# A two-layer decoder trunk: parameter loads placed behind the first step, inputs taken by feature halves, the first weights in smaller pieces

## The chip, the cores and the metric

The kernel runs on one core of one Trainium2 chip. The metric is device time in microseconds (us) for one execution of the whole program. A profiled execution gives a trace of every instruction and transfer. The engines are PE (TensorE), DVE (VectorE), ACT (ScalarE), POOL (GpSimd) and SP (SyncE, which here only issues transfers). PEld is PE's loading of stationary operands.

## The reference: what is computed

Two layers, each a half-step SwiGLU feed-forward block, then three causal mixers side by side, then a second half-step feed-forward block. All is float32; x is 256 tokens by 1024 features.

```python
def rms_norm(x, g):
    y = x * lax.rsqrt(jnp.mean(x * x, axis=-1, keepdims=True) + RMS_EPS)
    return y * g

def swiglu(h, w13, w2):                    # w13: 1024 x 5632, w2: 2816 x 1024
    g, u = jnp.split(h @ w13, 2, axis=-1)
    return (jax.nn.silu(g) * u) @ w2

for l in range(DEPTH):                     # DEPTH = 2
    x = x + 0.5 * swiglu(rms_norm(x, norm_ffn1[l]), ffn1_w13[l], ffn1_w2[l])
    h = rms_norm(x, norm_mix[l])
    z, xbc, dt_raw, cq, ckv, kidx, widx, xl, gl = jnp.split(h @ w_in[l], offsets, axis=-1)
    y_ssd = ssd_mixer(z, xbc, dt_raw, ..., ssd_a_log[l], ssd_d[l], ssd_norm[l])
    y_att = dsa_mixer(cq, ckv, kidx, widx, ...)
    y_lru = rglru_mixer(xl, gl, ...)
    x = x + jnp.concatenate([y_ssd, y_att, y_lru], axis=-1) @ w_out[l]
    x = x + 0.5 * swiglu(rms_norm(x, norm_ffn2[l]), ffn2_w13[l], ffn2_w2[l])
```

`ssd_d` holds one skip factor for each of 8 heads; the mixers use it, as most of the small parameters, only after the first feed-forward block.

## The kernel before

x stays in SBUF as two tiles `xr` of 128 tokens (h = 0, 1) by 1024 features. A norm block (`norm_block`, one for each token half h and feature half c) has four PE transposes into one PSUM tile, four pairs of ACT and DVE instructions that write a rounded part `xh` and a remainder `xl`, and one ACT pass `nsq` over the 128 x 512 inputs for the sum of squares. The row scale (`norm_end`) is applied later.

Every float32 product is three matmuls: whi by xh, wlo by xh, whi by xl. The weights are split on the chip (`wsplit`): ACT copies a 128 x 1024 piece to a rounded `whi`, and DVE subtracts to get `wlo`. Four pairs of `whi` and `wlo` are held at a time (pool `wsplit`, 4 buffers), and four raw tiles `wraw` of 1 MB.

The first feed-forward step `ffn(..., first=True)` runs over 11 column groups c. A group takes two raw tiles (q = 0, 1: rows 0 to 511 and 512 to 1023 of the weights), each by two transfers of 512 KB (t = 0: gate columns, t = 1: up columns); each raw tile is split in two pairs, and a pair feeds 12 matmuls (2 rows of 128 by 2 token halves by 3). Then `th_s` (tanh on ACT) and `hf` (DVE) make the gated product, which PE transposes. All weight and x transfers are issued by SP in program order. A transfer that is issued takes one of 8 completion semaphores of its kind in turn, and waits for the transfer that had it before.

The small parameters are loaded by `load_params`, called in the program at group c = 1: 28 transfers, issued by POOL, with 8 semaphores of their own. `derive_params`, called at c = 8, transposes the rows collected in `stA` and `stB` into columns and computes what the mixers need. The two `dcol` transfers pick every second element of `ssd_d`, so each moves single elements of 4 bytes, repeated for 64 partitions.

Engines run their instructions in order. The order on an engine is not the program's: a scheduler at build time places each instruction by its own estimate of when it can start, so loads that are late in the program but wait for nothing come early. `issue_after` tells it to hold an instruction behind another.

Of the kernel before, what the change touches and what calls it, by code (L numbers as in the profile page):

```python
# [7 lines left out]
F32 = mybir.dt.float32  # L8
# [3 lines left out]
ALU = mybir.AluOpType  # L12
# [3 lines left out]
P = 128  # L16
DEPTH = 2
SEQ = 256
NH = SEQ // P
D = 1024  # L20
KD = D // P
DFF = 2816
# [42 lines left out]
def tile_decoder_trunk(ctx: ExitStack, tc: tile.TileContext, A: dict, out: bass.AP):  # L65
    nc = tc.nc
    V, S, G, T = nc.vector, nc.scalar, nc.gpsimd, nc.tensor

    cp = Lined(ctx.enter_context(tc.tile_pool(name="const", bufs=1)))
# [9 lines left out]
    def small_ps():  # L79
        return psm.tile([P, 512], F32, name="sm")  # L80
# [16 lines left out]
    stage = sp0.enter_context(tc.tile_pool(name="stage", bufs=1))  # L97
    g1 = stage.tile([2 * KD, P], F32, name="g1")
    S.dma_start(g1, A["norm_ffn1"].rearrange("l (m p) -> (l m) p", p=P))
    for h in range(NH):  # L100
        for c in range(2):
            nc.sync.dma_start(X[h][:, c * 512:(c + 1) * 512], x_in[0, h * P:(h + 1) * P, c * 512:(c + 1) * 512])
    gcol1 = cp.tile([P, 2 * KD], F32, name="gcol1")
    pg1 = small_ps()
# [24 lines left out]
    def cols_of(name, l0, n):  # L129
        w, r0, _ = cols[name]  # L130
        return colT[w][:, r0 + l0:r0 + l0 + n]
# [4 lines left out]
    kg = cp.tile([P, DEPTH, 64], F32, name="kg")  # L136
    kig = cp.tile([P, DEPTH, 64], F32, name="kig")
    dcol = cp.tile([P, DEPTH, 4], F32, name="dcol")
    rope = cp.tile([P, NH, 2, 16], F32, name="rope")
    wbd = cp.tile([P, 2, DEPTH, 2, P], F32, name="wbd")  # L140
    a_neg = cp.tile([P, DEPTH, 8], F32, name="a_neg")
# [62 lines left out]
    def load_params(stage):  # L204

        stA = stage.tile([P, P], F32, name="stA")
        stB = stage.tile([P, P], F32, name="stB")
        for nm, (w, r0, n) in cols.items():
            src = A[nm]
            if len(src.shape) == 2:  # L210
                ap = src.rearrange("l (m p) -> (l m) p", p=P)
            else:
                ap = src.rearrange("l k (m p) -> (l k m) p", p=P)
            G.dma_start((stA if w == 0 else stB)[r0:r0 + DEPTH * n, :], ap)
        for t, nm, n in ((a_log, "ssd_a_log", 8), (dtb, "ssd_dt_bias", 8), (qg, "q_norm", 64), (kg, "k_norm", 64),
                         (kig, "kidx_norm", 64)):
            src = A[nm]
            G.dma_start(t, bass.AP(tensor=src.tensor, offset=src.offset, ap=[[0, P], [n, DEPTH], [1, n]]))
        for r in range(2):
            src = A["ssd_d"]  # L220
            G.dma_start(dcol[64 * r:64 * r + 64], bass.AP(tensor=src.tensor, offset=src.offset + r,
                                                          ap=[[0, 64], [8, DEPTH], [2, 4]]))
        G.dma_start(rope, A["rope"].rearrange("(h p) a c -> p h a c", p=P))
        G.memset(wbd, 0.0)
        for i, nm in enumerate(("lru_wa", "lru_wi")):
            src = A[nm]
            for r in range(2):
                for l in range(DEPTH):
                    G.dma_start(wbd[64 * r:64 * r + 64, i, l, :, 64 * r:64 * r + 64],
                                src[l, r::2].rearrange("b c d -> c b d"))  # L230
        return stA, stB

    def derive_params(stage, stA, stB):
        for i, (st, n) in enumerate(((stA, nA), (stB, nB))):
            pc = small_ps()
            T.transpose(pc[:, :n], st[:n, :], ident[:n, :n])
            V.tensor_copy(colT[i][:, :n], pc[:, :n])
        V.tensor_scalar(dcol, dcol, 0.5, None, ALU.mult)
        S.activation(a_neg, a_log, AF.Exp)
        V.tensor_scalar(a_neg, a_neg, -1.0, None, ALU.mult)  # L240
        nlam = stage.tile([P, 4], F32, name="nlam")
        V.tensor_scalar(nlam, cols_of("lru_lambda", 0, 4), -1.0, None, ALU.mult)
        lsp = stage.tile([P, 4], F32, name="lsp")
        softplus(lsp, nlam, stage, "ls")
        V.tensor_scalar(c8[:, 0], lsp, -8.0, None, ALU.mult)
        V.tensor_scalar(c8[:, 1], lsp, -4.0, None, ALU.mult)
        V.tensor_scalar(c8[:, 2], lsp, 4.0, None, ALU.mult)
        V.tensor_scalar(hb[:, 0], cols_of("lru_ba", 0, 4), 0.5, None, ALU.mult)
        V.tensor_scalar(hb[:, 1], cols_of("lru_bi", 0, 4), 0.5, None, ALU.mult)
# [67 lines left out]
    def ffn(n, w13, w2, pool, finish, first=False):  # L317
        rh_ = pool.tile([P, NH], F32, name="rhalf")
        V.tensor_scalar(rh_, n.r, 0.5, None, ALU.mult)
        rq = pool.tile([P, NH], F32, name="rquar")  # L320
        V.tensor_mul(rq, rh_, rh_)
        hh, hl = [], []
        for c in range(KF // 2):
            if first and c == 1:
                staged = load_params(pool)
            if first and c == 8:
                derive_params(pool, *staged)
            ps = [psg.tile([P, 512], F32, name="gu") for _ in range(NH)]
            for q in range(2):
                raw = rp.tile([P, 4, 512], F32, name="wraw")  # L330
                for t in range(2):
                    c0 = t * DFF + c * 256
                    nc.sync.dma_start(raw[:, :, t * 256:(t + 1) * 256],
                                      w13[q * 512:(q + 1) * 512, c0:c0 + 256].rearrange("(k p) c -> p k c", p=P))
                with tc.issue_after(n.last) if c == 1 else nullcontext():
                    ws = [wsplit([P, 2, 512], [(slice(None), raw[:, 2 * i:2 * i + 2])], V) for i in range(2)]
                for h in range(NH):
                    hs = slice(h * P, (h + 1) * P)
                    for k in range(4):
                        kk = 4 * q + k  # L340
                        mmt(ps[h], n.h[kk][:, hs], n.l[kk][:, hs], ws[k // 2][0][:, k % 2], ws[k // 2][1][:, k % 2],
                            kk == 0, kk == KD - 1)
            pt = small_ps()
            for h in range(NH):
                th = pool.tile([P, 256], F32, name="th_s", bufs=2)
                S.activation(th, ps[h][:, 0:256], AF.Tanh, scale=rh_[:, h:h + 1])  # L346
                V.scalar_tensor_tensor(th, th, 1.0, ps[h][:, 0:256], ALU.add, ALU.mult)  # L347
                hf = pool.tile([P, 256], F32, name="hf", bufs=2)
                V.tensor_mul(hf, th, ps[h][:, 256:512])
                for j in range(2):  # L350
                    T.transpose(pt[:, j * SEQ + h * P:j * SEQ + (h + 1) * P], hf[:, j * P:(j + 1) * P], ident)  # L351
            a = pool.tile([P, 2, SEQ], F32R, name="hh", bufs=KF // 2)
            b = pool.tile([P, 2, SEQ], F32R, name="hl", bufs=KF // 2)
            pt2 = pt.rearrange("p (a t) -> p a t", a=2)
            S.activation(a, pt2, AF.Copy)
            V.tensor_sub(b, pt2, a.bitcast(F32))
            for j in range(2):
                hh.append(a[:, j])
                hl.append(b[:, j])
        for c in range(2):  # L360
            acc = [psa.tile([P, 512], F32, name="acc") for _ in range(NH)]
            for k0, nk in ((0, 2), (2, 4), (6, 4), (10, 4), (14, 4), (18, 4)):
                raw = rp.tile([P, 4, 512], F32, name="wraw")
                nc.sync.dma_start(raw[:, :nk], w2[k0 * P:(k0 + nk) * P, c * 512:(c + 1) * 512]
                                  .rearrange("(k p) c -> p k c", p=P))
                ws = [wsplit([P, 2, 512], [(slice(None), raw[:, i:i + 2])], V) for i in range(0, nk, 2)]
                for h in range(NH):
                    hs = slice(h * P, (h + 1) * P)
                    for k in range(nk):
                        kk = k0 + k  # L370
                        mmt(acc[h], hh[kk][:, hs], hl[kk][:, hs], ws[k // 2][0][:, k % 2], ws[k // 2][1][:, k % 2],
                            kk == 0, kk == KF - 1)
                    if k0 + nk == KF:
                        xs = X[h][:, c * 512:(c + 1) * 512]
                        V.scalar_tensor_tensor(xs, acc[h], rq[:, h:h + 1], xs, ALU.mult, ALU.add)
                        finish(h, c)
# [461 lines left out]


    n = norm_begin()  # L840
    for h in range(NH):
        for c in range(2):
            norm_block(n, h, c, lambda m: gcol1[:, m:m + 1])
    norm_end(n)
    sp0.close()
# [88 lines left out]
```

## Time and profile before

| | |
|---|---|
| time, three runs | 1036.16, 1037.38, 1037.73 us, median 1037.38 |
| profiled execution | 1035.55 us, of which the profiled span is 1033.8 us |
| PE busy | 988.3 us of the span (96%) |
| DVE, ACT busy | 660.6 us (64%), 515.9 us (50%) |
| POOL busy | 52.6 us (5%), issues of transfers not counted |
| moved by transfers | 172.46 MB, mean 167 GB/s |
| mean granted TensorE clock | 0.991 |

Times in rows count from the start of the span. A busy share says how full an engine is over the whole span; a wait at one place shows only in the rows of that place, in brackets, as the idle time before an instruction and what ended it.

### The profile page before, as it was taken

The page shows a single profiled execution, that of the slowest core. Times are in us where ns is not written, and L with a number is a line of the kernel's source. Part 1 is how long each engine was busy: PE and PEld are TensorE (multiplying, and loading weights), DVE is VectorE, ACT ScalarE, POOL GpSimd, SP SyncE. Part 2 cuts the span into 40 slices and gives each one's busy share as a digit, 9 for nine tenths or more (in the row PEclk, how much of TensorE's full clock was granted, in tenths as well). Part 3 has the DMA queues.
Part 4 walks back from the last instruction along what each step waited for, and adds up shares of the span by engine and source line. Part 5 has one row for each costly group of instructions (what it writes and reads, how often), then busy time and mean ns, then how long its engine had stood idle before and what let it go on. Part 6 is the DMA issues. An engine that isn't in the chain of part 4 may idle for free.

```text
span 1033.8 us, 12880 instructions
## 1 busy us (share of the span) xinstructions
PE 988.3 (96%) x4819; PEld 803.8 (78%) x4819; DVE 660.6 (64%) x1157; ACT 515.9 (50%) x806; POOL 52.6 (5%) x133
## 2 busy tenths in 40 slices
PE   2999999999879999999999999999997899999998
PEld 1888888898854788888888888888897458888886
DVE  2656764567986666565566656555789766656543
ACT  4454544567741644444555544454695245454442
POOL 5100000005000000000000000000420000000000
PEclk9999999999989999999999999999999899999999
DMA  8865555564304565655665665567432166565560
GB/s 175 256 193 176 181 180 200 179 202 138 123 1 139 180 191 182 182 173 177 207 198 171 196 182 164 183 195 234 148 101 80 43 202 192 175 188 159 185 222 21
DMA packets 142719, 172.46 MB, mean 167 GB/s; under 512 B 4834, under 2 KB 114544, under 8 KB 142656
## 3 DMA queue, kind: packets, MB, share of 16 engines
q1 hardware_dynamic: 141728, 171.03, 51.9%
q0 software_dynamic: 896, 0.60, 1.0%
q8 instruction: 38, 0.62, 0.2%
q14 instruction: 25, 0.20, 0.1%
q10 hardware_dynamic: 32, 0.01, 0.0%
HBM read 170.57 MB, written 1.05 MB: 166 GB/s over the span
## 4 chain that ended last, share of the span: by engine, by line
PE 81%; DVE 9%; DMA 4%; ACT 3%; POOL 2%; issue 1%; SPq 0%; DVEq 0%; ACTq 0%; POOLq 0%
PE gu L267 16%; PE gu L268 16%; PE gu L269 16%; PE acc L267 8%; PE acc L269 8%; PE acc L268 8%; DMA wraw<-in_ffn_w_dram 4%; PE gu L802 3%; DVE wlo L262 2%; PE sm L351 2%; DVE xbc L669 2%; DVE score L537 1%; ACT whi L261 1%; PE sm L290 1%; DVE m L534 1%
## 5 line engine op out<-in xcount | busy, mean ns | idle before, releaser
L262 DVE TENSOR_TENSOR wlo<-wraw,whi 128x1024 fp32r<-128x1024 f32 (+1 forms) x304 | 370.3, 1220 | 270.3 <-ACT whi L261 262.2
L261 ACT ACTIVATE whi<-wraw 128x1024 fp32r<-128x1024 f32 (+1 forms) x304 | 321.7, 1061 | 294.3 <-PE gu L269 158.3
L267 PE MATMUL gu<-whi,xh 128*128 128x512 f32 (+1 forms) x736 | 290.4, 397 | 8.8 <-ACT whi L261 8.8
L269 PE MATMUL gu<-whi,xl 128*128 128x512 f32 (+1 forms) x736 | 289.2, 395 | 0.0
L268 PE MATMUL gu<-wlo,xh 128*128 128x512 f32 (+1 forms) x736 | 286.9, 391 | 0.0
L267 PEld LDWEIGHTS gu<-whi,xh 128*128 128x128 f32 x736 | 138.9, 189 | 34.8 <-ACT whi L261 9.2
L268 PEld LDWEIGHTS gu<-wlo,xh 128*128 128x128 f32 x736 | 138.9, 189 | 27.9 <-DVE wlo L262 0.8
L269 PEld LDWEIGHTS gu<-whi,xl 128*128 128x128 f32 x736 | 138.7, 188 | 27.3
L269 PE MATMUL acc<-whi,hl 128*128 128x512 f32 x352 | 137.7, 391 | 0.0
L268 PE MATMUL acc<-wlo,hh 128*128 128x512 f32 x352 | 137.1, 389 | 0.0
L267 PE MATMUL acc<-whi,hh 128*128 128x512 f32 x352 | 135.7, 391 | 0.0
L252 PE MATMUL gu<-xh,whi 128*128 128x256 f32 x256 | 75.6, 295 | 6.3 <-DVE z L768 4.0
L346 ACT ACTIVATE th_s<-gu,rhalf 128x256 f32<-128x256 f32 x88 | 41.8, 475 | 76.0 <-PE gu L269 76.0
L268 PEld LDWEIGHTS acc<-wlo,hh 128*128 128x128 f32 x352 | 66.1, 188 | 13.7
L269 PEld LDWEIGHTS acc<-whi,hl 128*128 128x128 f32 x352 | 66.1, 188 | 13.6
L267 PEld LDWEIGHTS acc<-whi,hh 128*128 128x128 f32 x352 | 66.1, 188 | 13.3
L253 PE MATMUL gu<-xl,whi 128*128 128x256 f32 x256 | 74.9, 293 | 0.0
L254 PE MATMUL gu<-xh,wlo 128*128 128x256 f32 x256 | 74.4, 291 | 0.0
L252 PEld LDWEIGHTS gu<-xh,whi 128*128 128x128 f32 x256 | 49.5, 193 | 8.4 <-issue 5.3
L347 DVE SCALAR_TENSOR_TENSOR th_s<-th_s,gu 128x256 f32<-128x256 f32 x88 | 36.7, 417 | 27.1 <-ACT th_s L346 27.1
L253 PEld LDWEIGHTS gu<-xl,whi 128*128 128x128 f32 x256 | 49.5, 193 | 1.8 <-issue 1.4
L254 PEld LDWEIGHTS gu<-xh,wlo 128*128 128x128 f32 x256 | 49.6, 194 | 1.0 <-issue 0.5
(306 smaller groups left out, 828.9 us busy)
## 6 DMA issues: line engine op xcount, KB each, us to landing
wraw<-in_ffn_w_dram SPq DMA_DIRECT2D x184, 512.0 KB, 4.8
wraw<-in_ffn_w_dram SPq DMA_DIRECT2D x40, 1024.0 KB, 5.0
wraw<-in_w_in_dram SPq DMA_DIRECT2D x16, 1024.0 KB, 5.2
wraw<-in_w_out_dram SPq DMA_DIRECT2D x8, 1024.0 KB, 5.0
wraw<-in_w_in_dram SPq DMA_DIRECT2D x4, 920.0 KB, 4.8
xr<-in_x_dram SPq DMA_DIRECT2D x4, 256.0 KB, 4.5
out_dram<-xr SPq DMA_DIRECT2D x4, 256.0 KB, 2.6
wq<-in_w_uq_dram SPq DMA_DIRECT2D x2, 256.0 KB, 6.6
```

Source lines behind the costliest of these rows:

```text
L252: T.matmul(o, lh, rh, start=first, stop=False)
L253: T.matmul(o, lh, rl, start=False, stop=False)
L254: T.matmul(o, ll, rh, start=False, stop=last)
L261: S.activation(hi[sl], raw, AF.Copy)
L262: eng.tensor_sub(lo[sl], raw, hi[sl].bitcast(F32))
L267: T.matmul(o, xh, wh, start=first, stop=False)
L268: T.matmul(o, xh, wl, start=False, stop=False)
L269: T.matmul(o, xl, wh, start=False, stop=last)
L346: S.activation(th, ps[h][:, 0:256], AF.Tanh, scale=rh_[:, h:h + 1])
L347: V.scalar_tensor_tensor(th, th, 1.0, ps[h][:, 0:256], ALU.add, ALU.mult)
L351: T.transpose(pt[:, j * SEQ + h * P:j * SEQ + (h + 1) * P], hf[:, j * P:(j + 1) * P], ident)
L802: T.matmul(acc, y[:, h * P:(h + 1) * P], w, start=t == 0, stop=t == len(ys) - 1)
```

## The change

The x blocks are loaded and normed with the feature half outermost. The first group's weights come in eight transfers of 256 KB instead of four of 512 KB. `load_params` is held behind a one-column POOL copy `mark` that reads `hf` of the first group. `ssd_d` is loaded as 8 contiguous values for each layer into all 128 partitions (`skip`), and two DVE instructions make `dcol` from it.

```diff
-    for h in range(NH):
-        for c in range(2):
+    for c in range(2):
+        for h in range(NH):
             nc.sync.dma_start(X[h][:, c * 512:(c + 1) * 512], x_in[0, h * P:(h + 1) * P, c * 512:(c + 1) * 512])
...
+    skip = cp.tile([P, DEPTH, 8], F32, name="skip")
...
-                         (kig, "kidx_norm", 64)):
+                         (kig, "kidx_norm", 64), (skip, "ssd_d", 8)):
             src = A[nm]
             G.dma_start(t, bass.AP(tensor=src.tensor, offset=src.offset, ap=[[0, P], [n, DEPTH], [1, n]]))
-        for r in range(2):
-            src = A["ssd_d"]
-            G.dma_start(dcol[64 * r:64 * r + 64], bass.AP(tensor=src.tensor, offset=src.offset + r,
-                                                          ap=[[0, 64], [8, DEPTH], [2, 4]]))
...
-        V.tensor_scalar(dcol, dcol, 0.5, None, ALU.mult)
+        for r in range(2):
+            rows = slice(64 * r, 64 * r + 64)
+            V.tensor_scalar(dcol[rows], skip[rows, :, r::2], 0.5, None, ALU.mult)
...
             if first and c == 1:
-                staged = load_params(pool)
+                mark = pool.tile([P, 1], F32, name="mark")
+                mark = G.tensor_copy(mark, hf[:, 0:1])
+                with tc.issue_after(mark.ins):
+                    staged = load_params(pool)
...
-                for t in range(2):
-                    c0 = t * DFF + c * 256
-                    nc.sync.dma_start(raw[:, :, t * 256:(t + 1) * 256],
-                                      w13[q * 512:(q + 1) * 512, c0:c0 + 256].rearrange("(k p) c -> p k c", p=P))
+                nk = 2 if first and c == 0 else 4
+                for k0 in range(0, 4, nk):
+                    for t in range(2):
+                        c0 = t * DFF + c * 256
+                        nc.sync.dma_start(raw[:, k0:k0 + nk, t * 256:(t + 1) * 256],
+                                          w13[q * 512 + k0 * P:q * 512 + (k0 + nk) * P, c0:c0 + 256]
+                                          .rearrange("(k p) c -> p k c", p=P))
...
-    for h in range(NH):
-        for c in range(2):
+    for c in range(2):
+        for h in range(NH):
             norm_block(n, h, c, lambda m: gcol1[:, m:m + 1])
```

POOL before, near its start (`a_log` to `rope` are parameters, `tri` and `inv` masks): ten rows, in which the loads begin at once.

```order
L218 DMA a_log<-in_ssd_a_log_dram 128x16
L849 AFFINE_SELECT tri<-ones 128x128
L218 DMA dtb<-in_ssd_dt_bias_dram 128x16
L218 DMA qg<-in_q_norm_dram 128x128
L218 DMA kg<-in_k_norm_dram 128x128
L857 AFFINE_SELECT inv_211<-inv_211 128x128
L218 DMA kig<-in_kidx_norm_dram 128x128
L221 DMA dcol<-in_ssd_d_dram 64x8x1 x2
L223 DMA rope<-in_rope_dram 128x2x32
L224 MEMSET wbd 128x1024
```

POOL in the change at the same place:

```order
L854 AFFINE_SELECT tri<-ones 128x128
L862 AFFINE_SELECT inv_212<-inv_212 128x128
L325 COPY mark<-hf 128x1
L215 DMA stA<-in_norm_mix_dram 16x128
L215 DMA stA<-in_norm_ffn_dram 16x128
L215 DMA stA<-in_ssd_conv_b_dram 16x128
L215 DMA stA<-in_ssd_norm_dram 8x128
L215 DMA stA<-in_cq_norm_dram 4x128
```

All 27 loads now stand behind `mark`; the twelve row loads come first, `a_log` is the 13th, `skip` the 18th.

ACT before, from its first pass over x to the third and fourth split of weights (`nsq`, `xh`: norm; `whi`: rounded weights):

```order
L297 ACTIVATE nsq,nss<-xr 128x512 x2
L293 ACTIVATE xh<-sm,gcol_102 128x128
L297 ACTIVATE nsq,nss<-xr 128x512
L239 ACTIVATE a_neg<-a_log 128x16
L293 ACTIVATE xh<-sm,gcol_102 128x128 x2
L297 ACTIVATE nsq,nss<-xr 128x512
L293 ACTIVATE xh<-sm,gcol_102 128x128 x6
L261 ACTIVATE whi<-wraw 128x1024 x2
L293 ACTIVATE xh<-sm,gcol_102 128x128 x3
L261 ACTIVATE whi<-wraw 128x1024 x2
```

ACT in the change at the same place:

```order
L296 ACTIVATE nsq,nss<-xr 128x512 x2
L292 ACTIVATE xh<-sm,gcol_102 128x128
L296 ACTIVATE nsq,nss<-xr 128x512
L292 ACTIVATE xh<-sm,gcol_102 128x128 x2
L296 ACTIVATE nsq,nss<-xr 128x512
L292 ACTIVATE xh<-sm,gcol_102 128x128 x3
L260 ACTIVATE whi<-wraw 128x1024
L292 ACTIVATE xh<-sm,gcol_102 128x128 x3
L260 ACTIVATE whi<-wraw 128x1024 x2
L292 ACTIVATE xh<-sm,gcol_102 128x128 x2
L260 ACTIVATE whi<-wraw 128x1024
```

Six `xh`, not nine, now precede the first `whi`, and `a_neg` has left the start.

ACT in the change where `a_neg` stands now, in the third and fourth column groups (`hh`: rounded transpose of `hf`):

```order
L260 ACTIVATE whi<-wraw 128x1024
L360 ACTIVATE hh<-sm 128x512
L260 ACTIVATE whi<-wraw 128x1024
L238 ACTIVATE a_neg<-a_log 128x16
L351 ACTIVATE th_s<-gu,rhalf 128x256
L260 ACTIVATE whi<-wraw 128x1024
```

It follows the 14th `whi` of the program and precedes the tanh of the third group; whatever it waits for, the `whi` behind it wait for too. On PE the transposes of the last norm block stand behind the first 14 matmuls of the feed-forward step instead of ahead of them. Behind the first 46 ACT, 70 DVE and 148 PE instructions the three engines run the same instructions in the same order as before, but for one swap of PE instructions late in the first step.

## Rows read from the trace of the kernel before

**Rows 1.** The profile's page: busy us (share) of engines; a group's busy, mean ns.

```profile
PE 988.3 (96%) x4819; PEld 803.8 (78%) x4819; DVE 660.6 (64%) x1157; ACT 515.9 (50%) x806; POOL 52.6 (5%) x133
...
L262 DVE TENSOR_TENSOR wlo<-wraw,whi 128x1024 fp32r<-128x1024 f32 (+1 forms) x304 | 370.3, 1220 | 270.3 <-ACT whi L261 262.2
```

**Rows 2.** Chain of waits, 0 to 60: start us, us, what.

```profile
2.63 0.43 SPq L333
3.11 18.46 DMA wraw<-in_ffn_w_dram
21.65 1.06 ACT whi L261
22.76 1.22 PE gu L267 x2
...
27.80 0.43 PE gu L267
...
33.52 0.23 PE gu L268
```

**Rows 3.** Stretch, its us; busy PE, PEld, DVE, ACT, POOL; clock; DMA share; GB/s.

```profile
2.00:4.00 2.00, 0.46 (x2) 0.40 (x3) 0.39 (x3) 0.96 (x3) 1.99 (x5) 1.00 0.85 283
4.00:6.00 2.00, 1.90 (x8) 1.20 (x7) 0.31 (x3) 1.46 (x5) 1.99 (x5) 1.00 0.54 154
14.00:16.00 2.00, 0.00 (x0) 0.00 (x0) 0.00 (x0) 0.00 (x0) 0.04 (x1) 1.00 2.17 7
24.00:26.00 2.00, 1.98 (x5) 1.59 (x6) 2.00 (x7) 1.49 (x4) 1.57 (x5) 1.00 1.10 349
```

**Rows 4.** Transfers of 0 to 30: what, issuer, count, KB each, us from issue to landing.

```profile
wraw<-in_ffn_w_dram SPq DMA_DIRECT2D x1, 512.0 KB, 8.4
...
wraw<-in_ffn_w_dram SPq DMA_DIRECT2D x1, 512.0 KB, 18.5
...
dcol<-in_ssd_d_dram POOLq DMA_DIRECT2D x2, 2.0 KB, 12.8
```

**Rows 5.** Timeline of ACT, 0 to 22: start us, us, line, operation, idle before.

```profile
3.76 0.63 ACT L297 ACTIVATE nsq<-xr 128x512 f32<-128x512 f32 x1 [1.03 <-DMA xr<-in_x_dram]
...
4.83 0.63 ACT L297 ACTIVATE nsq<-xr 128x512 f32<-128x512 f32 x1 [0.35 <-DMA xr<-in_x_dram]
...
7.21 0.63 ACT L297 ACTIVATE nsq<-xr 128x512 f32<-128x512 f32 x1 [1.40 <-DMA xr<-in_x_dram]
...
9.70 0.63 ACT L297 ACTIVATE nsq<-xr 128x512 f32<-128x512 f32 x1 [0.54 <-DMA xr<-in_x_dram]
...
10.33 1.95 ACT L293 ACTIVATE xh<-sm,gcol 128x128 fp32r<-128x128 f32 x6
```

**Rows 6.** Timeline of PE, 36 to 50, two transposes among matmuls.

```profile
39.25 0.39 PE L267 MATMUL gu<-whi,xh 128*128 128x512 f32 x1
39.48 0.38 PE L351 MATMUL sm<-ident,hf 128*128 128x128 f32 x2
39.62 0.47 PE L267 MATMUL gu<-whi,xh 128*128 128x512 f32 x1
39.93 0.39 PE L268 MATMUL gu<-wlo,xh 128*128 128x512 f32 x1
```

**Rows 7.** Timeline of POOL, 0 to 60: issues of parameter loads.

```profile
3.30 0.53 POOL L218 DMA_DIRECT2D qg<-in_q_norm_dram  x1
...
24.94 0.52 POOL L214 DMA_DIRECT2D stA<-in_lru_conv_w_dram  x1
```

**Rows 8.** Transfers as in Rows 4, of parameters.

```profile
stA<-in_norm_mix_dram POOLq DMA_DIRECT2D x1, 8.0 KB, 14.5
...
stA<-in_lru_conv_b_dram POOLq DMA_DIRECT2D x1, 2.0 KB, 5.6
```

**Rows 9.** Timeline of ACT, 20 to 60: the tanh of group 0 and the 14th whi.

```profile
37.18 0.48 ACT L346 ACTIVATE th_s<-gu,rhalf 128x256 f32<-128x256 f32 x1 [0.70 <-PE gu L269]
...
53.85 1.06 ACT L261 ACTIVATE whi<-wraw 128x1024 fp32r<-128x1024 f32 x1 [0.32 <-PE gu L269]
```
## Prediction, before the changed kernel ran

> **What bounds the kernel now.** I read the page first: PE is busy 96% of the span [rows 1], so whatever is to be gained lies where PE does not work. Next the chain of waits at the start: one weight transfer holds it for 18.46 us, from 3.11 to 21.57, ACT splits that piece at 21.65, and the first feed-forward matmul starts at 22.76 [rows 2]. From there the chain is PE's matmuls alone, and between 24 and 120 us PE waits for nothing that the profile shows. So the kernel is a late start followed by dense PE work, and a start that comes earlier moves all that follows, since the order behind it stays the same.
>
> Why is the transfer late? Two transfers of 512 KB, issued at 2.63 and 3.11 [rows 2], landed after 8.4 and 18.5 us [rows 4], so at 11.0 and 21.6. At the 349 GB/s that the stream reaches later [rows 3], 0.524 MB take 1.50 us. The second is therefore 9.0 us later than its size asks. Between 14 and 16 us almost nothing moves: 7 GB/s [rows 3]. The two `dcol` transfers, 2 KB each, were issued from 5.16 on and needed 12.8 us in the median [rows 4]; they fill that gap. They are the only ones made of single 4-byte elements. I read this as engines held by element-wise pieces, with weights queued behind them. The x blocks are late too: the four passes over x start at 3.76, 4.83, 7.21 and 9.70 [rows 5], while the moved bytes fall from 283 GB/s (2 to 4 us) to 154 (4 to 6) [rows 3], just when the first parameter loads run.
>
> **The change part by part.**
>
> *`dcol` without 4-byte pieces, loads behind `mark`.* This takes the 9.0 us gap away from the front, and the loads that slow x. What is late next? Transfers: by 4.0 us, 283 GB/s for 2 us have brought 0.57 MB; the other 0.48 MB of x at 349 GB/s arrive at 5.4, the first pair of 256-KB pieces (0.52 MB) at 6.9, and each further pair 1.5 us later: 8.4, 9.9, 11.4. ACT: from 3.76 it has four passes over x at 0.63 and, in the new order, six `xh` at 1.95 / 6 = 0.325 [rows 5], which is 4.47; I add 0.6 for waits on the second x block and on transposes (0.35 of it stands ahead of the second pass today). 3.76 + 4.47 + 0.6 = 8.8. The first pair has landed by then, so ACT, not the transfer, decides. With 1.06 for the split [rows 2] and 0.05 to PE, the first matmul starts at 9.9: 12.8 us earlier.
>
> *x by feature halves.* The first pair of weights meets features 0 to 255, so both token halves of that block are ready when it is split. The transposes of the last block move behind 14 matmuls. They are on the path now; two transposes and two matmuls take 39.25 to 39.93 = 0.68, less 2 x 0.23, so 0.11 for one [rows 6] and 0.45 for four: minus 0.4 from the gain.
>
> *Pieces of 256 KB.* Four more transfers for SP, whose issues (0.43 us [rows 2]) stay ahead of the 0.75 us that moving one takes. What they buy is that the first split needs 0.5 MB rather than 1 MB, 1.5 us; as ACT decides, I count it at nothing. It becomes worth 1.5 us if x and its norm turn out faster.
>
> *Slow matmuls.* Today the first 13 matmuls run at 0.43 us, up to 28.2, and later ones at 0.23 [rows 2], though the granted clock of those stretches reads 1.00 [rows 3]: the pace of the lower of TensorE's levels (1.2 GHz), after almost 9 us without work. In the change PE stands idle from the third block's transposes to 9.9, some 3 us. I count the same 13 slow matmuls. Bounds: all 13 fast would give 13 x 0.2 = 2.6 more; a second slow stretch after a gap costs as much. I take zero.
>
> *DVE in the first group.* Its subtractions (1.22 each [rows 1]), eight `xl` and the small norm steps now meet PE without the 9 us pause in which half of them ran before. From 9.9 on, four subtractions, seven `xl` about as long as an `xh` and some 1.2 for the norm's rest are 8.4 us, ready by 18.5; PE needs the fourth pair after 36 matmuls (5.5 us for 13, 23 x 0.23, 0.4 for transposes), at 21. Covered, by 2.5 us; a stall would cost its overshoot. Added: nothing, down to minus 1.
>
> *The loads at their new place.* `mark` reads `hf` of group 0. The second tanh of that group stands at 37.18 [rows 9], hence at 24.8 in the change, and `mark` at about 26. 27 issues at 0.52 [rows 7] follow, eight at a time, each later one waiting for a landing of 5.6 us [rows 8]. `a_log`, the 13th, is issued at about 34 and lands at 40; ACT's `a_neg`, behind the 14th split (53.85 [rows 9], so 41.4), runs at 42.5. `skip`, the 18th, lands near 44; DVE's `dcol` stands behind the 16th subtraction, near 48. Both come in time, if only by some us, and the weights have 349 GB/s against the mean of 167, so the loads cost nothing here. Price without that cover: the last rival.
>
> Sum: 12.8 - 0.4 = 12.4 us saved. Against the profiled execution, 1033.8 of span and 1.75 around it = 1035.55, that is 1023.15. This execution lies 1.8 us (0.2%) under the median of the three runs, 1037.38; from that the forecast is 1025.0.
>
> **A rule against the pieces.** The x blocks are 256 KB as well; the first two landed about 1.07 us apart [rows 5]. The Trainium skill, DMA: Bandwidth & Descriptors, section "Rules for kernel authors", wants at least 1 MiB per transfer, and its section "Anatomy of one DMA — SWDGE (gpsimd) path" fits 2.0 us plus bytes over 436 GB/s to each transfer that POOL issues. By that, as an estimate, a 256-KB piece would take 2.6 us if each waited for the one before. The trace does not agree for the first two blocks; it would for the last two. The second rival below has that case from rows.
>
> **A rule against the new place of the loads.** POOL's issue of a load took 0.53 us at 3.30 and 0.52 at 24.94 [rows 7], though DVE was busy 0.39 of 2.00 us in the first stretch and 2.00 of 2.00 in the second [rows 3]. The Trainium skill, SBUF — State Buffer, section "SBUF: two separate sides", warns that POOL cannot write descriptors while DVE holds a port they share. The trace shows no such delay for this DVE work; what it would feed is the last rival.
>
> **Rivals.**
>
> 1. *x stays as slow as now.* If parameter loads are not what slows x, the last pass still starts at 9.70; with 0.63, three `xh` and the split, matmuls begin at 12.4: 10.4 - 0.4 = 10.0 saved, 1027.4. For it: the weights share x's queue, and nothing here shows x without the loads. Against: the fall of GB/s falls together with the loads.
>
> 2. *Pieces come one at a time*, 2.45 us apart like the second to fourth x blocks. From 9.70, eight pieces end at 29.3; split, wait and the last 12 matmuls (1.06 + 0.4 + 2.75) bring group 0 to 33.5, against 36.2 now (28.2 + 35 x 0.23): 2.7 saved, 1034.7. Against it: 349 GB/s with queued 512-KB transfers.
>
> 3. *The pause is not `dcol`'s.* Then the change does not do what it says: a pause of 9.0 us stays, 12.4 - 9.0 = 3.4 saved, 1034.0. Against it: `dcol` is in flight for just that time, and no transfer of the start moves so little in so long.
>
> 4. *More*: PE's slow stretch shrinks with its idle time. Up to 2.6, of which the DVE chain lets some 2 through: 1023.0.
>
> 5. *Slower: the late loads block ACT and DVE.* If each landing takes 14.5 us, as that of `norm_mix` did [rows 8], `a_log` is issued at 43 and lands at 57.5. ACT, in order, stands still from 42.5. The 14 pairs split by then hold 168 matmuls: 9.9 + 5.5 + 155 x 0.23 = 51. PE then waits to 57.5 + 1.06, 7.6 us. `skip` lands at 70.5, DVE's next subtraction ends at 71.7, while PE has used the two pairs left at 58.6 + 5.5 = 64.1: 7.6 more. 15.2 lost against 12.4 won: 1040.2. It turns the sign from landings of some 13.5 us on. Against it: under full weight stream, without `dcol`, landings took 5.6.
>
> **How the numbers follow.** Forecast 63%, rival 1 15%, rival 2 5%, rival 3 4%, rival 4 9%, rival 5 4%. The forecast's own range is 1023.5 to 1027 (DVE's minus 1, the 0.6 of waits, and 0.8 for the spread of runs). With rivals 1 and 4 the range is 1022.5 to 1028.5; rivals 2, 3 and 5 and some tails, 15 to 20%, lie outside. A measurement here tells 0.2%, some 2 us, from no change. All cases but the last save more than that, with rivals 2 and 3 near enough to give 2% to no change: faster 0.95, same 0.02, slower 0.03.
>
> **What would show it.** Right: no stretch without bytes before 15 us; the last pass over x before 8; first feed-forward matmul at 9 to 11; no wait of PE over 0.5 us up to 60; `a_neg` on ACT without a wait for `a_log`; the span near 1021.4. Wrong: the first split waiting for a weight transfer (rivals 1 to 3), matmuls of 0.43 in more than one stretch, or ACT or DVE idle at 42 to 60 for `a_log` or `skip` (rival 5).

## The result, and the profile after

The changed kernel takes 1024.13 us (median of 4 runs, 1022.00 to 1025.87), the kernel before in the same comparison 1036.77 (4 runs, 1034.64 to 1037.73): ratio 0.9881, 95% interval 0.9863 to 0.99. It saves 12.6 us; 12.4 were forecast. Two later comparisons gave the same kernel 1022.35 and 1023.93.

The profiled execution of the changed kernel is its slowest, 1025.87 us with a span of 1024.1. The chain of waits at its start (start us, us, what) answers to [rows 2]:

```profile
1.70 4.72 DMA xr<-in_x_dram
...
6.51 0.72 ACT nsq L296 x2
...
9.00 1.08 ACT whi L260
...
10.12 1.22 PE gu L266 x2
...
13.03 0.43 PE gu L267
...
13.74 0.24 PE gu L267
...
15.36 0.44 PE sm L289 x4
```

The transfer of 18.46 us is gone from the chain. What ends last now is an x block (landed at 6.4), then ACT's work on x, then the first split. The first feed-forward matmul starts at 10.12 instead of 22.76. The matmuls keep the pace of 0.43 us only until 13.7, 3.6 us behind the first; before, it was 5.5 us (22.76 to 28.23). The four moved transposes stand at 15.36 with 0.44 us.

The stretches that answer to [rows 3], with columns as there:

```profile
2.00:4.00 2.00, 0.66 (x3) 0.60 (x4) 0.80 (x4) 1.17 (x3) 0.21 (x1) 1.00 0.89 302
4.00:6.00 2.00, 1.54 (x8) 1.05 (x6) 0.35 (x1) 1.26 (x5) 0.00 (x0) 1.00 0.85 233
6.00:8.00 2.00, 1.09 (x4) 0.71 (x4) 0.48 (x2) 1.49 (x5) 0.00 (x0) 1.00 1.01 332
14.00:16.00 2.00, 2.00 (x12) 1.65 (x12) 2.00 (x5) 0.90 (x3) 0.00 (x0) 1.00 1.09 385
```

Between 14 and 16 us 385 GB/s are moved instead of 7. The dip at 4 to 6 us has become smaller (233 instead of 154 GB/s), but it is still there, with no parameter load in flight. The passes over x on ACT's timeline answer to [rows 5]:

```profile
3.56 0.63 ACT L296 ACTIVATE nsq<-xr 128x512 f32<-128x512 f32 x1 [0.82 <-DMA xr<-in_x_dram]
...
4.42 0.63 ACT L296 ACTIVATE nsq<-xr 128x512 f32<-128x512 f32 x1
...
6.51 0.63 ACT L296 ACTIVATE nsq<-xr 128x512 f32<-128x512 f32 x1 [1.11 <-DMA xr<-in_x_dram]
...
7.64 0.62 ACT L296 ACTIVATE nsq<-xr 128x512 f32<-128x512 f32 x1
```

The last starts at 7.64 instead of 9.70, yet the third still waits 1.11 us for its block. The late loads, on the timelines of POOL, then ACT, then DVE, each with the instruction that reads what was loaded:

```profile
27.54 0.19 POOL L325 COPY mark<-hf 128x1 f32<-128x1 f32 x1 [25.33 <-DVE hf L354]
...
35.37 0.57 POOL L219 DMA_DIRECT2D a_log<-in_ssd_a_log_dram  x1
...
38.05 0.53 POOL L219 DMA_DIRECT2D skip<-in_ssd_d_dram  x1
```

```profile
43.28 0.20 ACT L238 ACTIVATE a_neg<-a_log 128x16 f32<-128x16 f32 x1
```

```profile
49.25 0.34 DVE L237 TENSOR_SCALAR dcol<-skip 64x8 f32<-64x8 f32 x2
```

`a_log` and `skip` are issued at 35.37 and 38.05 and land after 2.8 and 6.6 us by the table of transfers, so at 38.2 and 44.7. Their readers run at 43.28 and 49.25 and show no wait in brackets. From 9 to 120 us PE waited for one thing (us in total, times, longest), the start itself:

```profile
PE gu L266 <- ACT whi L260: 2.5, 1, 2.5
```

How much of the start is kept? ACT splits 304 pairs of weights in one order in both kernels, so the same split can be followed. The 61st (late in the first step) and the 304th, first in the kernel before, then in the changed one:

```profile
189.54 1.06 ACT L261 ACTIVATE whi<-wraw 128x1024 fp32r<-128x1024 f32 x1
...
1018.88 1.06 ACT L261 ACTIVATE whi<-wraw 128x1024 fp32r<-128x1024 f32 x1 [0.30 <-PE acc L269]
```

```profile
176.60 1.06 ACT L260 ACTIVATE whi<-wraw 128x1024 fp32r<-128x1024 f32 x1
...
1009.47 1.06 ACT L260 ACTIVATE whi<-wraw 128x1024 fp32r<-128x1024 f32 x1 [0.30 <-PE acc L268]
```

The lead is 12.94 and 9.41 us. The start won 12.9; the mixers and the long stretches behind them gave back 3.5 in this execution. Whether that belongs to the change is asked below. The lead at the 61st split, "the front" from here on, is the best measure of what a change of the start is worth. Each front is one profile against the one profile of the kernel before; the ratios of the times below are against the kernel before on the same chip.

| kernel | first feed-forward matmul, us | front, us | median us | ratio, 95% interval |
|---|---|---|---|---|
| only_skip | 13.82 | -9.51 | 1028.51 | 0.9919, 0.9905 to 0.9934 |
| only_behind | 11.62 | -11.32 | 1024.66 | 0.9886, 0.987 to 0.9903 |
| double_pieces | 33.69 | +11.27 | 1046.23 | 1.0087, 1.0056 to 1.0118 |
| whole_pieces | 11.57 | -11.04 | 1025.70 | 0.9893, 0.9874 to 0.9913 |
| token_halves | 10.09 | -12.31 | 1024.13 | 0.9879, 0.9858 to 0.9899 |
| changed kernel | 10.12 | -12.94 | 1024.13 | 0.9881, 0.9863 to 0.99 |
| after_again | 9.72 | -12.28 | 1022.35 | 0.9866, 0.9845 to 0.9887 |
| after_third | 9.88 | -12.54 | 1023.93 | 0.9883, 0.9868 to 0.9899 |
| weights_first | 9.17 | -13.72 | 1020.14 | 0.9846, 0.9824 to 0.9869 |
| weights_first_again | 9.21 | -13.92 | 1020.29 | 0.9845, 0.9831 to 0.9858 |

### The profile page after: what moved, and what is told of

The parts are those of the page before. It is cut to its first block, busy times and chain, and to the rows that moved or that the text cites. A ratio compares the mean times of both kernels' runs of the same rounds, so it can differ in the third digit from the quotient of the medians.

```text
span 1024.1 us, 12885 instructions
## 1 busy us (share of the span) xinstructions
PE 991.1 (97%) x4819; PEld 806.0 (79%) x4819; DVE 661.3 (65%) x1158; ACT 515.2 (50%) x806; POOL 52.7 (5%) x133
## 3 DMA queue, kind: packets, MB, share of 16 engines
HBM read 170.57 MB, written 1.05 MB: 168 GB/s over the span
## 4 chain that ended last, share of the span: by engine, by line
PE 83%; DVE 9%; ACT 3%; DMA 2%; POOL 2%; issue 1%; SPq 0%; ACTq 0%; DVEq 0%; POOLq 0%
PE gu L266 16%; PE gu L268 16%; PE gu L267 16%; PE acc L267 8%; PE acc L268 8%; PE acc L266 8%; PE gu L807 3%; DVE wlo L261 2%; DMA wraw<-in_ffn_w_dram 2%; PE sm L356 2%; DVE xbc L674 1%; PE gu L251 1%; DVE score L542 1%; PE gu L253 1%; PE gu L252 1%; PE sm L289 1%
## 5 line engine op out<-in xcount | busy, mean ns | idle before, releaser
L267 PEld LDWEIGHTS acc<-wlo,hh 128*128 128x128 f32 x352 | 66.1, 188 | 13.7
```

The source lines that it names most:

```text
L267: T.matmul(o, xh, wl, start=False, stop=False)
```

## The experiments

### One part alone: the 4-byte pieces, or the place

Of the kernel before, **only_skip** takes the new form of the load and leaves all loads early:

```diff
-        for r in range(2):
-            src = A["ssd_d"]
-            G.dma_start(dcol[64 * r:64 * r + 64], bass.AP(tensor=src.tensor, offset=src.offset + r,
-                                                          ap=[[0, 64], [8, DEPTH], [2, 4]]))
...
+        for r in range(2):
+            rows = slice(64 * r, 64 * r + 64)
+            V.tensor_scalar(dcol[rows], skip[rows, :, r::2], 0.5, None, ALU.mult)
```

> Before, with one edit: ssd_d loaded as contiguous 8 values (skip) instead of two transfers of 4-byte elements; all loads stay at the front, x by token halves, 512-KB pieces. Theory (the 4-byte elements hold the transfer engines and the second weight transfer behind them): the pause of 9 us goes, the second 512-KB transfer lands near 12.6, ACT's last xh ends at 12.3, first feed-forward matmul at 13.5 to 14, time some 9 us under before (about 1028). Rival (any early load holds the weights): first matmul at 20 or later, time 1034 or more.

**only_behind** moves all loads and keeps the 4-byte pieces:

```diff
-                staged = load_params(pool)
+                mark = pool.tile([P, 1], F32, name="mark")
+                mark = G.tensor_copy(mark, hf[:, 0:1])
+                with tc.issue_after(mark.ins):
+                    staged = load_params(pool)
```

> Before, with one edit: the loads stand behind mark; the two transfers of 4-byte elements are kept and so move to about 40 us. Theory (they hold the engines there as well, but the weights are some 10 us ahead of PE by then): first matmul near 11.3, a pause of 7 to 9 us in the moved bytes somewhere between 36 and 52 us, PE waits under 1 us for it, time about 11.5 us under before (1025). Rival (the pause costs wherever it falls): PE waits 5 to 8 us between 45 and 70, time about 1032.

Without the 4-byte pieces, and with nothing else changed, the first split on ACT's timeline of only_skip waits 1.81 us for its weights; in [rows 2] it started at 21.65:

```profile
12.72 2.00 ACT L260 ACTIVATE whi<-wraw 128x1024 fp32r<-128x1024 f32 x2 [1.81 <-DMA wraw<-in_ffn_w_dram]
```

The start is 8.9 us earlier for two transfers of 2 KB. The pause was theirs. The other early loads slow x as well: with them, in only_skip, 143 GB/s are moved from 4 to 6 us and the third pass over x waits for its block until 7.11; without them, in only_behind, it is 262 GB/s, and the third pass starts at 5.54 without a wait. (The fourth pass of only_skip, at 8.34, waited for no block; it stood behind ACT's own work.)

only_behind starts another 2.2 us earlier. Its `dcol` transfers are as slow at their new place. The stretch while they are in flight (columns as in [rows 3]), and the transfers issued from 36 to 42 (as in [rows 4]):

```profile
41.00:46.00 5.00, 5.00 (x25) 4.08 (x24) 3.13 (x4) 3.18 (x5) 3.47 (x6) 1.00 0.85 2
```

```profile
wraw<-in_ffn_w_dram SPq DMA_DIRECT2D x2, 512.0 KB, 15.0
...
dcol<-in_ssd_d_dram POOLq DMA_DIRECT2D x2, 2.0 KB, 11.4
```

For 5 us 2 GB/s are moved (from 40 to 49 no stretch of 1 us moves more than 31), and two weight transfers need 15 us; PE is busy for all of the 5 us, and up to 120 it waits for no weights. The raw tiles loaded ahead cover the pause. So either edit takes the pause off the path, and their gains don't add: -9.5 and -11.3 alone, against -11.0 for both together without the smaller pieces (whole_pieces, below, which also has the new order of x).

### Twice the suspected cost

**double_pieces** loads `dcol` a second time into a tile that nothing reads, early as before:

```diff
-        for r in range(2):
+        for t, r in ((dcol, 0), (dcol, 1), (dcol2, 0), (dcol2, 1)):
```

> Before, with the two transfers of 4-byte elements issued twice, the second time into a tile that nothing reads. Theory (each such pair holds the engines some 8 to 9 us): the pause grows by that, first matmul at about 31, time about 1045. Rival (the pause has another cause, the pieces only wait in it): first matmul within 1 us of 22.8, time within 2 us of before.

Its first split, and two of the empty stretches:

```profile
32.58 2.00 ACT L262 ACTIVATE whi<-wraw 128x1024 fp32r<-128x1024 f32 x2 [18.68 <-DMA wraw<-in_ffn_w_dram]
```

```profile
14.00:16.00 2.00, 1.12 (x4) 0.72 (x4) 0.81 (x6) 0.00 (x0) 0.00 (x0) 1.00 1.18 11
20.00:22.00 2.00, 0.00 (x0) 0.00 (x0) 0.00 (x0) 0.00 (x0) 0.51 (x1) 1.00 1.35 5
```

The queue of POOL's transfers from 14 to 22 us (packets, MB, share of the time of 16 transfer engines):

```profile
q0 software_dynamic: 57, 0.00, 91.2%
```

The split is 10.9 us later than before (32.58 against 21.65) for two more such transfers, 5.5 each and so more than the 8 to 9 for both that were expected; removing two gained 4.5 each. The bytes stop (11 and 5 GB/s) while 57 packets from POOL's queue, with next to no bytes, hold the transfer engines for 91% of the time. Why such a packet takes so long no run shows. The third rival is refuted from both sides.

### The pieces, and the halves of x

In the changed kernel, **whole_pieces** puts the 512-KB pieces back:

```diff
-                nk = 2 if first and c == 0 else 4
+                nk = 4
```

> The changed kernel with the first group's weights in four transfers of 512 KB again. As predicted (ACT decides the start, the pieces are worth little): nine xh instead of six precede the first split in its order, first matmul near 11.2, second tanh of group 0 later by 0.3 to 1 us, time later by at most 1 us. Rival (each transfer pays a fixed time, larger ones are better): weights land earlier, first matmul at or before 10.1, time 0 to 1 us less.

```profile
10.46 2.00 ACT L260 ACTIVATE whi<-wraw 128x1024 fp32r<-128x1024 f32 x2 [0.27 <-DMA wraw<-in_ffn_w_dram]
```

The first split starts at 10.46, ended by a transfer, where three profiles of the changed kernel have 9.00, 8.60 and 8.77, ended by ACT's own work. The front is -11.04 against -12.94, -12.28 and -12.54 (mean -12.59): the pieces are worth some 1.5 us. At most 1 us of the time was expected; the median is 3.4 us above that of after_again beside it, with intervals that overlap, and 1.6 to 1.8 above the other two medians of the changed kernel. The built order differs with the pieces: nine `xh`, not six, precede the first split here and end at 10.19, so the transfer ends a wait of only 0.27 us. With six ahead ACT would have been free near 9, and the split would still have had to wait for the landing at 10.4.

**token_halves** takes x by token halves again:

```diff
-    for c in range(2):
-        for h in range(NH):
+    for h in range(NH):
+        for c in range(2):
...
```

(the same two lines, at the loads and at the norm blocks)

> The changed kernel with x loaded and normed by token halves again. Theory (only the order of the first 48 matmuls is touched): first matmul near 10.1 as its six xh are those of token half 0; token half 1 follows later, PE waits up to 1 us in the first group, second tanh of group 0 later by 0 to 1.5 us. Rival (feature halves are what lets PE start early): first matmul 2 us later or PE waits of 2 us and more.

The first matmul at 10.09 and the front of -12.31 lie among the three of the changed kernel. The second tanh of group 0 came at 25.29, earlier than the 26.1 to 26.8 of the changed kernel and not later, as was expected; at the front nothing of it is left. The median is 1.8 us above that of after_again beside it and equal to that of the first comparison. The order of x is worth nothing that can be told.

### The changed kernel again, and weights ahead of x

The wait that is left is on x. In **weights_first** the first pair of 256-KB weight pieces is issued between the two feature halves of x:

```diff
     for c in range(2):
         for h in range(NH):
             nc.sync.dma_start(X[h][:, c * 512:(c + 1) * 512], x_in[0, h * P:(h + 1) * P, c * 512:(c + 1) * 512])
+        if c == 0:
+            load_w13(raw0, A["ffn1_w13"][0], 0, 0, 0, 2)
...
-                raw = rp.tile([P, 4, 512], F32, name="wraw")
+                raw = raw0 if head and q == 0 else rp.tile([P, 4, 512], F32, name="wraw")
```

> The changed kernel with the first pair of 256-KB pieces issued between the two feature halves of x. Theory (the split waits for ACT's norm work, which now partly follows it, and for landings): the pair lands near 7.35, where the third and fourth transfer land today, split at 7.4 to 8.5; PE has the third block's transposes ahead, so first matmul at 8.7 to 9.3, second tanh of group 0 earlier by 0.5 to 1.5 us, time 0.5 to 1.5 us less. Rival (DVE and ACT work of the norm bounds the first group anyway): first matmul earlier, second tanh within 0.4 us, time the same.

> The changed kernel once more, as base for the three beside it. Both theories: ratio to before 0.986 to 0.990, first matmul within 0.3 us of 10.1; the mixers may take some 2 us more or less than in the first profile.

Both ran once more, side by side on another chip:

> The changed kernel with the first pair of 256-KB weight pieces issued between the two feature halves of x, a second time, to tell it from the changed kernel on one chip. If its lead of 1.4 us at the front (first feed-forward matmul 9.17 instead of 9.7 to 10.1, and a shift of ACT and DVE against the kernel before of -13.9 instead of -12.4 to -13.1 at 50 to 100 us) is real, that shift comes out between -13.3 and -14.4 again, and the time about 1 us (0.5 to 2) under that of the changed kernel beside it. Rival, the lead is the spread of a run's slow first matmuls and mixers: a shift of -12.4 to -13.1 and a time within 0.5 us of the changed kernel's.

> The changed kernel as it is, beside the one with weights first. First feed-forward matmul between 9.7 and 10.2 us; the shift of ACT and DVE against the kernel before at 50 to 100 us between -12.4 and -13.1; time 1022 to 1025. If the number of first matmuls at 0.43 us is chance (8 in one profile of this kernel, more in the other), it comes out anywhere from 6 to 14 here; if the shorter idle time ahead shrinks it, as the fourth rival had it, it stays at 9 or fewer.

The chain at the start of weights_first_again:

```profile
2.68 5.66 DMA xr<-in_x_dram
...
8.47 1.09 PE sm L300 x4
9.56 0.85 PE gu L277 x2
```

The split is off the chain; a late x block and its transposes lead straight into the matmuls, 0.5 to 0.9 us earlier than in the changed kernel. The front is 1.4 us better than that of after_third beside it, and the time 3.6 us better (1020.29 against 1023.93; the intervals of the ratios, 0.9831 to 0.9858 and 0.9868 to 0.9899, don't touch). On the first chip the front of weights_first is better by 1.4 us than that of after_again as well, and the time by 2.2 (1020.14 against 1022.35; there the intervals overlap). Both are more than the 1 us expected. The rest, 0.8 and 2.2 us, comes behind the front. There the built program has another order on PE: four matmuls `acc<-ident,xbc` that stood behind the output matmuls stand ahead of them. PE's waits there, after_third first (207 to 317), then weights_first_again (275 to 292):

```profile
PE sm L623 <- DVE ya L619: 5.1, 1, 5.1
PE acc L745 <- DVE xbc L681: 2.1, 1, 2.1
```

```profile
PE acc L767 <- DVE xbc L689: 4.8, 1, 4.8
PE sm L631 <- DVE ya L627: 1.8, 1, 1.8
```

The two waits are 7.2 us together in the one and 6.6 in the other, which explains 0.6 of the 2.2. The eight output matmuls behind them take 6.44 us in the profile of after_third (shown below), and 1.9 less here:

```profile
290.80 4.57 PE gu L815 x8
```

Of that, 1.5 is the spread of executions, as the other two profiles of the changed kernel have 4.88 and 4.90 there. No run has the early weights without this other order, so what the order itself is worth is open. It is the fastest kernel found here: it beats the kernel before on both chips, and the changed one clearly on one of the two.

**What the mixers give back.** From the 61st to the last split the three profiles of the changed kernel gave back 3.5, gave back 1.5 and gained 0.6 us, with the same instructions in the same order. Two places show how. Behind PE's wait of 5.1 us for `ya`, eight output matmuls follow; their rows in the chains of the kernel before, after_third and the changed kernel's first profile:

```profile
304.88 5.26 PE gu L802 x8
```

```profile
292.39 6.44 PE gu L807 x8
```

```profile
294.35 4.88 PE gu L807 x8
```

And the granted clock (third column from the end) in two halves of that row, in the kernel before and in after_third:

```profile
304.88:307.50 2.62, 2.62 (x3) 1.18 (x4) 2.16 (x4) 1.63 (x3) 0.00 (x0) 0.50 0.00 0
307.50:310.14 2.64, 2.64 (x8) 1.21 (x7) 0.00 (x0) 0.00 (x0) 0.00 (x0) 0.89 0.00 0
```

```profile
292.39:295.60 3.21, 3.21 (x4) 1.50 (x5) 2.17 (x4) 1.62 (x3) 0.00 (x0) 0.50 0.00 0
295.60:298.83 3.23, 3.23 (x7) 1.29 (x6) 0.00 (x0) 0.00 (x0) 0.00 (x0) 0.64 0.00 0
```

After the same wait the lower level (0.50, 1.2 GHz) lasts longer in one execution than in the other, 1.2 us in this row. The first profile, which gave back most, lost nothing there. It lost 2.4 us earlier: at the 80th split its lead is 10.5 (11.6 again at the 101st; the last 2.1 are lost later, and what took them was not followed). PE waited 1.1 us for `adt` there, up to 231.02 (the cause is in the last section), and then ran at the lower level for a while, which after_third, with a wait of 0.3, did not; the stretch from 232 to 236 in the one and the other:

```profile
232.00:236.00 4.00, 4.00 (x23) 4.00 (x23) 3.16 (x7) 1.06 (x1) 2.33 (x6) 0.59 0.57 200
```

```profile
232.00:236.00 4.00, 4.00 (x37) 4.00 (x36) 3.38 (x7) 2.23 (x5) 2.79 (x7) 1.00 0.70 239
```

Three executions of one program differ by 4.1 us behind the front and lie on both sides of the kernel before, so nothing of this give-back can be put down to the change.

## Why the prediction was right

**The pause and what is late next.** Right in place and size. It put the 9 us to `dcol`; only_skip removed them and gained 9.5, double_pieces added 10.9. It said that ACT would decide and the first matmul start at 9.9; three profiles show 10.12, 9.72 and 9.88. But ACT decided by little. The second of the first pair of pieces, issued at 3.12, needed (what, issuer, count, KB, us from issue to landing)

```profile
wraw<-in_ffn_w_dram SPq DMA_DIRECT2D x1, 256.0 KB, 5.6
```

and landed at 8.7 (8.5 and 8.7 in the other two profiles), where the prediction had 6.9; the first split started at 9.00 (8.60, 8.77). Of 1.9 us of margin 0.1 to 0.3 were left, and had the pieces come only a little later, the transfer would have decided.

**The landing of x was mis-sized.** The step "the other 0.48 MB of x at 349 GB/s arrive at 5.4" failed: the last block landed at 7.35 (7.1 and 7.2 in the other two profiles). The third pass waited for its block to 6.5, and the fourth started at 7.64 (7.2, 7.3). Most of that is the order of the bytes. Up to 7.35, with columns as in [rows 3]:

```profile
0.00:7.35 7.35, 2.99 (x13) 2.37 (x13) 1.31 (x6) 4.03 (x10) 1.56 (x10) 1.00 0.67 210
```

That is 1.54 MB, of which x is 1.05; some 0.5 MB of weights, by this estimate, had moved among x, worth 1.4 us at 349 GB/s, while the prediction let x move first and the weights after it. The rest is the dip in moved bytes at 4 to 6 us. It was put down to the parameter loads; it is milder without them, but does not need them, and what makes it is open. The sum survived because ACT had work until the fourth block was there (in one of the three it waited 0.24 us for it), and because its waits stayed near the 0.6 us added for them: 9.00 - 3.56 - 4.47 = 0.97, and 0.59 and 0.71 in the other two. That the weights, late by 1.6 to 1.8 us like x, still landed just ahead of the split was luck, as no step of the prediction had reckoned with it. The first rival (x as slow as now) had its premise half right and its price wrong.

**Pieces of 256 KB: counted at nothing, worth some 1.5.** This follows from the x step. With x landing later, the second 512-KB piece would land behind ACT's work (10.46 against 9.00 in the first split); the smaller ones do not. The prediction named 1.5 us as the worth if x turned out faster; it is worth that because x, and the weights with it, turned out slower. The total came out right because the forecast held a start that whole pieces would not have reached. The Trainium skill, DMA: Bandwidth & Descriptors, section "Rules for kernel authors", asks for at least 1 MiB per transfer where bandwidth is the goal. That would speak for the larger pieces; here the measured sign is the other, and while the smaller pieces landed, from 8 to 12 us, 372 to 384 GB/s were moved.

**Slow matmuls: near enough on the mean.** The pace of 0.43 us lasted 5.5 us before, and 3.6, 5.9 and 5.0 (mean 4.8) in the three profiles. That this is the lower clock, as the prediction reads it, no row shows: the granted clock from 10 to 14 us reads 1.00. At (1 - 0.23 / 0.43) that is worth +0.9, -0.2 and +0.2 us. With it the front closes: 12.64 + 0.9 - 0.45 = 13.1 (12.94 measured), 13.04 - 0.2 - 0.45 = 12.4 (12.28), 12.88 + 0.2 - 0.45 = 12.6 (12.54). The fourth rival, a slow stretch that shrinks with the idle time, fits the first profile alone; the same kernel shows 3.6 and 5.9.

**DVE and the late loads.** Right: no wait of PE behind the first matmul up to 120 us, `a_neg` at 43.28 (42.5 forecast) and `dcol` at 49.25 (48) without waits. `mark` ran 1.5 us later than forecast, as the second tanh of group 0 came at 26.1 and not at 24.8. `a_log` landed faster than the 5.6 us taken (2.8), `skip` slower (6.6), and the margins were 5.1 and 4.6 us. The fifth rival was not tested at its condition, 13.5 us for each landing; in only_behind single transfers took 11 to 15 us and PE did not wait.

**The transposes** cost the 0.45 forecast (0.44 at 15.36), and the order of x that moved them gives nothing measurable in return.

**The total.** 12.4 forecast, 12.6 by medians, 12.3 to 12.9 at the front. The profiled span of 1024.1 is 2.7 above the 1021.4 named as a sign. Behind the POOL delay below, with the lower clock that followed it, 2.4 us were lost, of which 1.0 came back, and the rest was lost later; the other two profiles have 1020.6 and 1022.5.

## What to carry to other kernels

Look at the first 20 us for a stretch in which the transfers are in flight and move nothing; a few KB of 4-byte elements held half a MB of weights for 9 us here, and moving them to a place with buffered weights was enough, whatever their form. At a cold start size the first pieces by what the first instruction needs, and issue the first weights ahead of the input that is needed later. When two edits remove the same wait, test each alone: their gains do not add.

## What was not expected of the hardware

A small POOL operation took until the end of a DVE subtraction that started beside it. In the profile of the changed kernel, first POOL, then DVE:

```profile
227.56 0.25 POOL L155 TENSOR_SCALAR stt<-spc 128x16 f32<-128x16 f32 x1
...
228.34 1.42 POOL L155 TENSOR_SCALAR stt<-spc 128x16 f32<-128x16 f32 x1
```

```profile
228.43 1.22 DVE L261 TENSOR_TENSOR wlo<-wraw,whi 128x1024 fp32r<-128x1024 f32 x1
```

The operation that takes 0.25 us takes 1.42 beside the subtraction. In this execution the subtraction hit an earlier link of the chain to `adt` than in the others (in after_third the last one ahead of `adt`, which took 1.29 us there and 0.81 here), and PE waited 1.1 us for `adt` instead of 0.2 to 0.3. The Trainium skill, SBUF — State Buffer, section "SBUF: two separate sides", describes an exclusive lock on a port pair between such a DVE operation with two inputs in SBUF and a POOL operation that reads SBUF; this trace agrees in that one of the two waits, though no run here took either away to show it. By that section whichever starts first holds the pair; by the recorded starts that was POOL, by 0.09 us, and yet POOL waited.
